# A hybrid attention and recurrence layer on one core: VectorE blocks kept in written order, and token projections that go one weight tile at a time

## The chip, the cores and the metric

The kernel runs on one core of a Trainium2 chip. The metric is the device time of one execution in microseconds (us); lower is better. Engines are named as in the profile: PE is TensorE's matmuls, PEld its weight loads, DVE is VectorE, ACT is ScalarE, POOL is GpSimd, SP is SyncE, which here issues nearly all DMAs.

## The reference, cut to what matters

One layer over 512 tokens of width 1024, in float32. The input is normalised and projected once; the columns of that projection feed two branches.

```python
xn = rmsnorm(h, norm_gain[i])
proj = xn @ w_in[i]
aq, ak, av, ag, bq, bf, bi, bg, gate_a, gate_b = jnp.split(proj, split_pts, axis=-1)
# attention: 8 heads of 64, QK norm, relative bias, causal within blocks
qa, ka = rmsnorm(heads(aq), q_norm_gain[i]), rmsnorm(heads(ak), k_norm_gain[i])
ya = moba_attention(qa, ka, va, rel_bias)...
ya = (ya * silu(ag)) @ w_up_a[i]
# recurrence: 4 heads, key and value width 128
log_f = log_sigmoid(fpre) + log1p(lb * exp(min(-fpre, 30)))
kb, qb, vb = (1 - lb) * sigmoid(-fpre), silu(bq), bi
#   cum = cumsum(log_f); scores[t, s] = sum_k q[t] k[s] exp(cum[t] - cum[s]); plus a carried state
yb = rmsnorm(hgrn2_chunkwise(qb, kb, vb, log_f), hgrn_out_gain[i])
yb = (yb * silu(bg)) @ w_up_b[i]
merged = sigmoid(gate_a) * ya + sigmoid(gate_b) * yb
h = h + merged @ w_out[i]
h = h + (p[i] @ w_ple[i]) * sigmoid(h @ w_ple_gate[i])
```

## The kernel before, in words

Every float32 operand of a large matmul is split into a high half (`wh`, `xh`, made by ACT, L184) and a low half (`wl`, `xl`, the DVE subtraction in L185), and a product is three matmuls: high by high, high by low, low by high. A weight tile is 128x1024 (512 KB): SP loads it into one of two buffers `wf`, and ACT and DVE write its halves into one of three buffers each (`wh`, `wl`). So the tile three further on may be written only when PE has read the last of this one. Weight tiles are numbered in the order of their use: 0 to 3 are `bi`, 4 to 7 `av`, 8 and 9 the first head's `bf` and `bq`, 10 to 13 `aq`, 14 to 17 `ak`, and so on.

A token projection (`proj_tok`: `bi`, `av`, `aq`, `ak`) has four PSUM banks, one for each 128 tokens (`t` from 0 to 3), and eight k slices of 128, two in each of four weight tiles. All projections take their banks in turn from one pool of four (`mm`). A bank's next user waits until the last reader of its old contents is done: `av` gets the banks of `bi`, which ACT evicts into `biv` (L397); `aq` gets two banks of `av` and then those of `bf` and `bq` of the first head. `bf` has its last reader in L422 of `hgrn_gates`. `bq` has its last reader in L431, the query gate `qm = sigmoid(bq) * bq` (tile `hq`).

For `bi`, the first projection, a function `between` feeds the tiles one by one. The other three take two tiles at a time: first all 24 matmuls of banks 0 and 1 on both tiles, then those of banks 2 and 3. One matmul of 128x512 is one row of the PE's order.

PE's order is the written one: a small clock in the program (`tick`, `cost`, `yield`) lets generators for the recurrence, the attention and the normalisation put their matmuls between those of the projections. On DVE, ACT, POOL and SP a list scheduler sets the order, by priority (`tc.high_priority(offset=AHEAD)` moves a block ahead) and by when it believes operands to be ready; inside `tc.manual_schedule(engines=...)` the program sets the order for the engines named.

The recurrence runs a head at a time: `hgrn_gates` (sigmoids, the scan `cum` in L428, the query gate), then `hgrn_intra`: first subtractions of `cum` (L447, L448, L460, L481, L484, L510), an `Exp` on ACT, a product on DVE, then small matmuls into two banks (`lpb`, `lpa`), from which DVE builds `s32` (L539 and seven predicated copies, L496) and ACT writes other parts of `sc`; four POOL copies (L556) bring `s32` into `sc`. Then `hgrn_out`: `hktp` (transposes), `hds` (the state), `hop` (the output, which reads `sc`), `hms` (its norm).

Of the kernel before, what the change touches and what calls it, by code (L numbers as in the profile page):

```python
# [14 lines left out]
AF = mybir.ActivationFunctionType  # L15
OP = mybir.AluOpType
# [5 lines left out]
NT = S // 128  # L22
# [18 lines left out]
LD = 2  # L41
# [9 lines left out]
AHEAD = 150  # L51
# [6 lines left out]
def hybrid_layer_kernel(  # L58
# [106 lines left out]
    eye = mkf[:, 0:32]  # L165
# [14 lines left out]
        A.activation(lb[:, 5], lb[:, 4], AF.Ln)  # L180


    def split(hi, lo, src):
        A.activation(hi, src, AF.Copy)  # L184
        V.tensor_tensor(lo, src, hi.bitcast(F32), op=OP.subtract)  # L185
# [36 lines left out]
    def w_split(upto):  # L222
        while len(wtile) <= min(upto, len(wseq) - 1):
            i = len(wtile)
            w_load(i)
            ap, kn, cols = wseq[i]
            hi = unit("wh", f"wh{i}", R, (128, kn, cols))
            lo = unit("wl", f"wl{i}", R, (128, kn, cols))
            with tc.high_priority(offset=AHEAD):
                split(hi, lo, wraw[i])  # L230
            wtile.append((hi, lo))

# [135 lines left out]
    def proj_tok(g, name, xh, xl, between=None):  # L368
        banks = [bank("mm", f"{name}{t}") for t in range(NT)]
        for kp in range(4):  # L370
            if between:
                between(kp)
                w2 = [weight(w_tok[g, kp], 0)]
                order = [(0, kk, t) for kk in range(2) for t in range(NT)]
                if kp == 3:
                    order = [(0, kk, t) for t in range(NT) for kk in range(2)]
            elif kp % 2 == 0:
                w2 = [weight(w_tok[g, kp]), weight(w_tok[g, kp + 1])]
                order = [(k2, kk, t) for t in (0, 1) for k2 in range(2) for kk in range(2)]
                order += [(k2, kk, t) for t in (2, 3) for k2 in range(2) for kk in range(2)]  # L380
            else:
                continue
            for k2, kk, t in order:
                wh, wl = w2[k2]
                k = 2 * (kp + k2) + kk
                s_ = slice(t * 128, t * 128 + 128)
                for i, (a, b) in enumerate(((xh[k], wh), (xl[k], wh), (xh[k], wl))):
                    PE.matmul(banks[t], a[:, s_], b[:, kk, :], start=(k == 0 and i == 0),  # L388
                              stop=(k == KD - 1 and i == 2))
                tick(0.681)  # L390
        return banks
# [19 lines left out]
    def hgrn_gates(h, F, Q):  # L411
        a = unit("H", f"ha{h}")
        A.activation(a, F, AF.Abs)
        A.activation(a, a, AF.Exp, scale=-1.0)
        A.activation(a, a, AF.Ln, bias=onec[:, 0:1])
        um = unit("H", f"hu{h}")
        V.tensor_scalar(um, F, -1.0, 30.0, op0=OP.mult, op1=OP.min)
        A.activation(um, um, AF.Exp)
        A.activation(um, um, AF.Ln, bias=onec[:, 0:1], scale=lbv[:, h:h + 1])
        V.scalar_tensor_tensor(a, F, 0.0, a, op0=OP.min, op1=OP.subtract)  # L420
        kb = unit("H", f"hk{h}")
        V.tensor_tensor(kb, a, F, op=OP.subtract)  # L422
        A.activation(kb, kb, AF.Exp, bias=ln1mlb[:, h:h + 1])
        V.tensor_tensor(a, a, um, op=OP.add)
        cum = um
        for c in range(NT):
            s_ = slice(c * 128, c * 128 + 128)
            V.tensor_tensor_scan(cum[:, s_], onec.to_broadcast([128, 128]), a[:, s_], 0.0, OP.mult, OP.add)  # L428
        sigmoid(a, Q)
        qm = unit("QM", f"hq{h}", shape=(128, 16, 48))  # L430
        V.tensor_tensor(qm[:, :, 0:32], a.rearrange("p (g t) -> p g t", t=32), Q.rearrange("p (g t) -> p g t", t=32),  # L431
                        op=OP.mult)
        hg[h] = (kb, qm, cum)

    def hgrn_intra(h):
# [3 lines left out]
        def halves(b):  # L439

            x = unit("Q", f"hx{h}_{b}")
            n = S // (2 * b)

            def v(t, half):
                return t.rearrange("p (n two b) -> p n two b", two=2, b=b)[:, :, half, :]
            ref = v(cum, 0)[:, :, b - 1:b].to_broadcast([128, n, b])
            V.tensor_tensor(v(x, 0), ref, v(cum, 0), op=OP.subtract)  # L447
            V.tensor_tensor(v(x, 1), v(cum, 1), ref, op=OP.subtract)  # L448
            A.activation(x, x, AF.Exp)
            V.tensor_tensor(v(x, 0), v(kb, 0), v(x, 0), op=OP.mult)  # L450
            xq = x.rearrange("p (n two g t) -> p n two g t", two=2, t=32, g=b // 32)[:, :, 1]
            qq = q.rearrange("p (n two g) t -> p n two g t", two=2, g=b // 32)[:, :, 1]
            V.tensor_tensor(xq, qq, xq, op=OP.mult)
            return x

        def near():

            c2 = cum.rearrange("p (g n two) -> p g n two", n=16, two=2)
            o = qm[:, :, 32:48]
            V.tensor_tensor(o, c2[:, :, :, 1], c2[:, :, :, 0], op=OP.subtract)  # L460
            A.activation(o, o, AF.Exp)
            V.tensor_tensor(o, q.rearrange("p g (n two) -> p g n two", two=2)[:, :, :, 1], o, op=OP.mult)

        def fours(b):


            kx = unit("Q", f"hkx{h}_{b}")
            qx = unit("QX", f"hqx{h}_{b}", shape=(128, 16, 48))
            n, m = S // (4 * b), 8 // b
            parts = [(d, 4 - d, e * b) for d, e in ((1, 0), (2, 3), (3, 5))]  # L470
            k4 = kx.rearrange("p (n f t) -> p n f t", f=4, t=b)
            c4 = cum.rearrange("p (n f t) -> p n f t", f=4, t=b)
            b4 = kb.rearrange("p (n f t) -> p n f t", f=4, t=b)
            q4 = q.rearrange("p g (m f t) -> p g m (f t)", m=m, f=4)
            x4 = qx.rearrange("p g (m e) -> p (g m) e", m=m)
            y4 = qx.rearrange("p g (m e) -> p g m e", m=m)
            G.memset(k4[:, :, 3, :], 0.0)

            def end(w):
                return c4[:, :, 0:w, b - 1:b].to_broadcast([128, n, w, b])  # L480
            V.tensor_tensor(k4[:, :, 0:3], end(3), c4[:, :, 0:3], op=OP.subtract)  # L481
            for d, w, e in parts:
                o = x4[:, :, e:e + w * b].rearrange("p n (f t) -> p n f t", t=b)
                V.tensor_tensor(o, c4[:, :, d:4], end(w), op=OP.subtract)  # L484
            A.activation(k4[:, :, 0:3], k4[:, :, 0:3], AF.Exp)
            A.activation(qx, qx, AF.Exp)
            V.tensor_tensor(k4[:, :, 0:3], b4[:, :, 0:3], k4[:, :, 0:3], op=OP.mult)
            for d, w, e in parts:
                o = y4[:, :, :, e:e + w * b]
                V.tensor_tensor(o, q4[:, :, :, d * b:4 * b], o, op=OP.mult)  # L490
            return kx, qx
# [15 lines left out]
        kd = unit("KT", f"hkd{h}", shape=(128, 3 * 128))  # L507
        cv = cum.rearrange("p (c t) -> p c t", c=NT)
        k3 = kd.rearrange("p (c t) -> p c t", c=3)
        V.tensor_tensor(k3, cv[:, 0:3, 127:128].to_broadcast([128, 3, 128]), cv[:, 0:3, :], op=OP.subtract)  # L510
        A.activation(kd, kd, AF.Exp)
        V.tensor_tensor(kd, kd, kb[:, :3 * 128], op=OP.mult)
        yield 2.5
# [22 lines left out]
            PE.matmul(lnr[p_, c, :], kb[:, o:o + 32], qm[:, 4 * c + g, :], start=True, stop=True)  # L536
        cost(1.5)
        A.activation(cum, cum, AF.Exp)
        V.tensor_tensor(s32, lnr[:, :, 0:32], eye[:, None, :].to_broadcast([128, NT, 32]), op=OP.mult)  # L539
        scv = sc.rearrange("p (i two) t -> p i two t", two=2)  # L540
        for par in range(2):
            i = 64 * par
            A.activation(scv[0:64, :, par, 64:128], big[i:i + 64, 0:2, :], AF.Copy)
            for half in range(2):
                j = 64 * half
                A.activation(scv[j:j + 32, :, par, j + 32:j + 64], big[i + 32 * half:i + 32 * half + 32, 2:4, 0:32], AF.Copy)
        for i, b in ((4, 8), (1, 2)):
            for d, e in ((1, 0), (2, 3), (3, 5)):
                pred(i + d - 1, lambda t: t.rearrange("p c (m e) -> p c m e", m=8 // b)[:, :, :, d * b:4 * b],
                     l4[b].rearrange("p c (m e) -> p c m e", m=8 // b)[:, :, :, e * b:(e + 4 - d) * b])  # L550
        pred(0, lambda t: t.rearrange("p c (n two) -> p c n two", two=2)[:, :, :, 1], lnr[:, :, 32:48])
        q12 = q[:, 4:16]
        V.tensor_tensor(q12, q12, cum[:, 128:].rearrange("p (g t) -> p g t", t=32), op=OP.mult)
        for g in range(4):
            s_ = slice(32 * g, 32 * g + 32)
            G.tensor_copy(sc[s_, :, s_], s32[s_])  # L556
        hg[h] += (kd,)

    def hgrn_out(h, vb):
        kb, qm, cum, kd = hg[h][:4]  # L560
        nk = 3 * 128
        yield 3.5
        kt = bank("g", f"hktp{h}")
        for c in range(3):
            PE.transpose(kt[:, c * 128:c * 128 + 128], kd[:, c * 128:c * 128 + 128], ident)
# [449 lines left out]
```

## Time and profile before

| | |
|---|---|
| device time, median of 3 runs | 473.75 us (473.31 to 473.81) |
| device time of the profiled execution | 474.0 us |
| its span, first to last instruction | 471.9 us |
| PE busy | 464.6 us (98%), 2776 records |
| DVE busy | 310.8 us (66%), 615 instructions |
| ACT busy | 273.9 us (58%), 479 instructions |
| POOL busy | 14.2 us (3%), 34 instructions |
| HBM read | 45.75 MB |

A matmul's end is modelled in the profile, and its rows overlap: a row of 0.39 us starts 0.227 us after the one before it. The distance between starts is what shows PE's rate. "Idle before" in brackets counts from the modelled end, so a wait is longer by some 0.16 us when it is measured from start to start. Times below are us from the start of the span.

### The profile page before, as it was taken

To read this page: it belongs to the slowest core of one execution; us is meant where nothing else is said; L and a number is where in the kernel's file an instruction comes from. 1 tells how busy PE (TensorE), PEld (TensorE's weight loads), DVE (VectorE), ACT (ScalarE), POOL (GpSimd) and SP (SyncE) were. 2 spreads that over 40 slices of the span, in tenths; PEclk is the share of its full clock that TensorE was granted. 3 is DMA by queue.
4 is the path that set the end of the run, shared out by engine and by line. 5 is a ranking of instruction groups with operands and counts; after the bars stand their busy time and mean duration, and the time that the engine had idled before them with its cause. 6 is when DMAs were issued, how large, how long until landed. Compare 5 with 4: busy or idle time off the path is not lost.

```text
span 471.9 us, 7256 instructions
## 1 busy us (share of the span) xinstructions
PE 464.6 (98%) x2776; PEld 384.8 (82%) x2776; DVE 310.8 (66%) x615; ACT 273.9 (58%) x479; POOL 14.2 (3%) x34
## 2 busy tenths in 40 slices
PE   9999999999999999999999999999999999999996
PEld 7888877888888778888788888888878888888886
DVE  4769696668989799849995466434459854543332
ACT  5857683478598789748885676554344522243201
POOL 0005000000000010000000100000000000000000
PEclk9999999999999999999999999999999999999999
DMA  7642222221541423231422233112534544322211
GB/s 228 218 145 90 90 89 90 89 90 50 172 145 59 141 85 90 90 111 47 131 91 92 90 101 102 47 62 53 188 95 138 193 145 147 109 93 95 91 44 46
DMA packets 19027, 50.42 MB, mean 107 GB/s; under 512 B 2352, under 2 KB 2992, under 8 KB 18992
## 3 DMA queue, kind: packets, MB, share of 16 engines
q1 hardware_dynamic: 18848, 49.95, 33.1%
q8 instruction: 22, 0.36, 0.3%
q14 instruction: 13, 0.11, 0.1%
q10 hardware_dynamic: 144, 0.01, 0.0%
HBM read 45.75 MB, written 2.10 MB: 101 GB/s over the span
## 4 chain that ended last, share of the span: by engine, by line
PE 87%; DVE 6%; ACT 5%; issue 1%; POOL 0%; DVEq 0%; POOLq 0%
PE ga L246 9%; PE g L246 9%; PE h L246 9%; PE gb L246 7%; PE bi L388 5%; PE ua L246 5%; PE ak L388 5%; PE ub L246 5%; PE av L388 5%; PE bg L246 5%; PE bf L246 4%; PE ag L246 3%; PE aq L388 3%; PE pe L246 2%; PE o L733 2%; PE s L700 2%
## 5 line engine op out<-in xcount | busy, mean ns | idle before, releaser
L184 ACT ACTIVATE wh<-wf 128x1024 fp32r<-128x1024 f32 (+1 forms) x81 | 77.5, 957 | 106.0 <-PE h L246 19.1
L185 DVE TENSOR_TENSOR wl<-wf,wh 128x1024 fp32r<-128x1024 f32 (+1 forms) x81 | 89.8, 1111 | 48.4 <-ACT wh L184 47.9
L707 DVE CUSTOM_DVE_ANT_0 p<-s,bias 128x128 f32<-128x128 f32 (+3 forms) x32 | 15.0, 486 | 21.8 <-PE s L700 21.7
L709 ACT ACTIVATE p<-p,ps 128x128 f32<-128x128 f32 (+3 forms) x32 | 17.7, 554 | 19.5 <-DVE ps L707 19.5
L246 PE MATMUL g<-hh,wh 128*128 128x512 f32 (+1 forms) x72 | 26.3, 365 | 0.0
L246 PE MATMUL g<-hl,wh 128*128 128x512 f32 (+1 forms) x72 | 26.3, 365 | 0.0
L246 PE MATMUL g<-hh,wl 128*128 128x512 f32 (+1 forms) x72 | 26.3, 365 | 0.0
L246 PE MATMUL gb<-xh,wh 128*128 128x512 f32 x64 | 26.3, 411 | 0.0
L246 PE MATMUL ga<-xh,wh 128*128 128x512 f32 x64 | 25.6, 400 | 0.0
L246 PE MATMUL gb<-xh,wl 128*128 128x512 f32 x64 | 25.1, 393 | 0.0
L246 PE MATMUL ga<-xh,wl 128*128 128x512 f32 x64 | 25.0, 391 | 0.0
L246 PE MATMUL gb<-xl,wh 128*128 128x512 f32 x64 | 25.0, 391 | 0.0
L246 PE MATMUL ga<-xl,wh 128*128 128x512 f32 x64 | 25.0, 390 | 0.0
L246 PE MATMUL h<-mh,wh 128*128 128x512 f32 x64 | 24.9, 390 | 0.0
L246 PE MATMUL h<-ml,wh 128*128 128x512 f32 x64 | 24.9, 389 | 0.0
L246 PE MATMUL h<-mh,wl 128*128 128x512 f32 x64 | 24.9, 389 | 0.0
L722 ACT ACTIVATE ptS<-pt 128x384 f32<-128x384 f32 (+1 forms) x24 | 12.5, 521 | 10.0 <-PE pt L718 9.8
L903 DVE TENSOR_TENSOR hf<-h,xres 128x512 f32<-128x512 f32 x8 | 5.5, 691 | 18.1 <-PE h L246 18.1
L246 PEld LDWEIGHTS g<-hh,wh 128*128 128x128 f32 x72 | 13.6, 189 | 2.2
L246 PEld LDWEIGHTS g<-hh,wl 128*128 128x128 f32 x72 | 13.6, 189 | 2.2
L246 PEld LDWEIGHTS g<-hl,wh 128*128 128x128 f32 x72 | 13.6, 189 | 2.1
L945 DVE TENSOR_TENSOR sg<-sg,pe 128x512 f32<-128x512 f32 (+1 forms) x9 | 5.6, 625 | 14.4 <-ACT sg L944 12.1
(319 smaller groups left out, 1265.2 us busy)
## 6 DMA issues: line engine op xcount, KB each, us to landing
wf<-in_w_tr_dram SPq DMA_DIRECT2D x32, 512.0 KB, 3.4
wf<-in_w_tok_dram SPq DMA_DIRECT2D x15, 512.0 KB, 3.3
wf<-in_w_up_dram SPq DMA_DIRECT2D x16, 256.0 KB, 2.7
wf<-in_w_o_dram SPq DMA_DIRECT2D x8, 512.0 KB, 3.3
wf<-in_w_g_dram SPq DMA_DIRECT2D x8, 512.0 KB, 3.3
bias<-in_brow_dram SPq DMA_DIRECT2D x8, 256.0 KB, 3.4
xres<-in_xT_dram SPq DMA_DIRECT2D x8, 256.0 KB, 2.8
xr<-in_xT_dram SPq DMA_DIRECT2D x7, 256.0 KB, 5.5
```

The source lines that it names most:

```text
L184: A.activation(hi, src, AF.Copy)
L185: V.tensor_tensor(lo, src, hi.bitcast(F32), op=OP.subtract)
L246: PE.matmul(ps, a[:, k, :], b[k], start=(n == 0), stop=(n == tot - 1))
L388: PE.matmul(banks[t], a[:, s_], b[:, kk, :], start=(k == 0 and i == 0), stop=(k == KD - 1 and i == 2))
L700: PE.matmul(sp[:, o:o + nk], qn[h][:, qs], k_[:, :nk], start=(i == 0), stop=(i == 1))
L707: V.tensor_tensor_reduce(p_, sp[:, o:o + nk], T[:, nk - 1::-1], -1.0, 3e38, OP.add, OP.min, st[:, 0:1])
L709: A.activation(p_, p_, AF.Exp, bias=st[:, 0:1], scale=-1.0, accum_out=st[:, 1:2])
L722: A.activation(pt, tp[:, :n * 128], AF.Copy)
L733: PE.matmul(o[64 * j:64 * j + 64, qs], va[kb][:, h0:h0 + 64], pts[2 * hp + j, i][:, o0 + kb * 128:o0 + kb * 128 + 128], start=(kb == 0), s ...
L903: V.tensor_tensor(t, ps, xres, op=OP.add)
L945: V.tensor_tensor(t[:, :w], t[:, :w], pe[:, s_], op=OP.mult)
```

## The change: three edits in the order of work

1. `proj_tok` takes one weight tile at a time also for `av`, `aq` and `ak`. The order inside a tile is k slice by k slice over all four banks; the last tile goes bank by bank.
2. A helper `in_order()` puts a few DVE instructions under `tc.manual_schedule`: the low halves of the weight tiles, the query gate, and the recurrence's first subtractions.
3. The end of `hgrn_intra` (from L539 to the POOL copies) gets high priority, with the product on `q12` (L553) moved behind the copies in the text; `hgrn_out` begins 5.0 us of the program's clock after it where it had 3.5.

```diff
+    def in_order():
+        return tc.manual_schedule(engines={mybir.EngineType.DVE})
...
-            with tc.high_priority(offset=AHEAD):
+            with tc.high_priority(offset=AHEAD), in_order():
                 split(hi, lo, wraw[i])
...
         for kp in range(4):
             if between:
                 between(kp)
-                w2 = [weight(w_tok[g, kp], 0)]
-                order = [(0, kk, t) for kk in range(2) for t in range(NT)]
-                if kp == 3:
-                    order = [(0, kk, t) for t in range(NT) for kk in range(2)]
-            elif kp % 2 == 0:
-                w2 = [weight(w_tok[g, kp]), weight(w_tok[g, kp + 1])]
-                order = [(k2, kk, t) for t in (0, 1) for k2 in range(2) for kk in range(2)]
-                order += [(k2, kk, t) for t in (2, 3) for k2 in range(2) for kk in range(2)]
-            else:
-                continue
-            for k2, kk, t in order:
-                wh, wl = w2[k2]
-                k = 2 * (kp + k2) + kk
+            wh, wl = weight(w_tok[g, kp], 0 if between else LD)
+            order = [(kk, t) for kk in range(2) for t in range(NT)]
+            if kp == 3:
+                order = [(kk, t) for t in range(NT) for kk in range(2)]
+            for kk, t in order:
+                k = 2 * kp + kk
...
-        V.tensor_tensor(qm[:, :, 0:32], a.rearrange("p (g t) -> p g t", t=32), Q.rearrange("p (g t) -> p g t", t=32),
-                        op=OP.mult)
+        with in_order():
+            V.tensor_tensor(qm[:, :, 0:32], a.rearrange("p (g t) -> p g t", t=32),
+                            Q.rearrange("p (g t) -> p g t", t=32), op=OP.mult)
...
-            V.tensor_tensor(v(x, 0), ref, v(cum, 0), op=OP.subtract)
-            V.tensor_tensor(v(x, 1), v(cum, 1), ref, op=OP.subtract)
+            with in_order():
+                V.tensor_tensor(v(x, 0), ref, v(cum, 0), op=OP.subtract)
+                V.tensor_tensor(v(x, 1), v(cum, 1), ref, op=OP.subtract)
...
         A.activation(cum, cum, AF.Exp)
-        V.tensor_tensor(s32, lnr[:, :, 0:32], eye[:, None, :].to_broadcast([128, NT, 32]), op=OP.mult)
+        with tc.high_priority(offset=AHEAD):
+            V.tensor_tensor(s32, lnr[:, :, 0:32], eye[:, None, :].to_broadcast([128, NT, 32]), op=OP.mult)
...
+            for g in range(4):
+                s_ = slice(32 * g, 32 * g + 32)
+                G.tensor_copy(sc[s_, :, s_], s32[s_])
         q12 = q[:, 4:16]
         V.tensor_tensor(q12, q12, cum[:, 128:].rearrange("p (g t) -> p g t", t=32), op=OP.mult)
-        for g in range(4):
-            s_ = slice(32 * g, 32 * g + 32)
-            G.tensor_copy(sc[s_, :, s_], s32[s_])
...
-        yield 3.5
+        yield 5.0
```

`near`, `fours` and the subtraction into `hkd` (L460, L481, L484, L510) get the same `in_order()` as the two lines shown.

Where the instructions stand. First PE, at the start of `aq` (banks `aq0` to `aq3`; `wh10` and `wh11` are the first two of its four weight tiles, `xh0` to `xh7` the k slices). Before:

```order
L388 MATMUL aq0_618<-wh10_536,xh0_390 128x512
...
L388 MATMUL aq0_618<-wh11_567,xh2_399 128x512
...
L388 MATMUL aq1_619<-wh10_536,xh0_390 128x512
...
L388 MATMUL aq2_620<-wh10_536,xh0_390 128x512
...
L388 MATMUL aq3_621<-wh10_536,xh0_390 128x512
```

Twelve rows lie from the first row of a bank to that of the next, so bank 3 is first written by the 37th matmul of `aq`. In the change (its lines stand three higher there):

```order
L385 MATMUL aq0_651<-wh10_560,xh0_399 128x512
L385 MATMUL aq0_651<-wh10_560,xl0_400 128x512
L385 MATMUL aq0_651<-wl10_561,xh0_399 128x512
L385 MATMUL aq1_652<-wh10_560,xh0_399 128x512
L385 MATMUL aq1_652<-wh10_560,xl0_400 128x512
L385 MATMUL aq1_652<-wl10_561,xh0_399 128x512
L385 MATMUL aq2_653<-wh10_560,xh0_399 128x512
L385 MATMUL aq2_653<-wh10_560,xl0_400 128x512
L385 MATMUL aq2_653<-wl10_561,xh0_399 128x512
L385 MATMUL aq3_654<-wh10_560,xh0_399 128x512
```

Bank 3 is now first written by the tenth matmul, bank 2 by the seventh. `av` and `ak` change in the same way.

Second DVE, in the first head, from the scan to the query gate. This is the change; the rows before read the same but for the line numbers (L510, L185, L484, L460, L512, L431):

```order
L425 SCALAR_TENSOR_TENSOR hu0_630<-onec_85,ha0_626 128x128 x4
L512 TENSOR_TENSOR hkd0_936<-hu0_630 128x384
L189 TENSOR_TENSOR wl12_658<-wf12_655,wh12_657 128x1024
L446 TENSOR_TENSOR hx0_64_713<-hu0_630 128x4x64
...
L485 TENSOR_TENSOR hqx0_8_820<-hu0_630 128x16x8
L460 TENSOR_TENSOR hq0_646<-hu0_630 128x16x16
L514 TENSOR_TENSOR hkd0_936<-hkd0_936,hk0_635 128x384
L429 TENSOR_TENSOR hq0_646<-ha0_626,bq0_601 128x16x32
```

The last row is the query gate, the last reader of `bq0`. It stands behind the same sixteen instructions as before: nothing moved here.

Third DVE, in the third head (`hq2`), where `s322` is that head's `s32` and `hqx3` and `hkd3` belong to the fourth. Before, from the fifth to the last of its seven predicated copies:

```order
L496 COPY_PREDICATED s322_1904<-mkf_69,lpa2_2185 128x16x4
...
L484 TENSOR_TENSOR hqx3_8_2612<-hu3_2336 128x16x8
L707 ISA p32_2301,ps32_2302<-s32_2298,bias3_1712 128x384
L460 TENSOR_TENSOR hq3_2352<-hu3_2336 128x16x16
L510 TENSOR_TENSOR hkd3_2705<-hu3_2336 128x384
L496 COPY_PREDICATED s322_1904<-mkf_69,lpa2_2185 128x16x2
L185 TENSOR_TENSOR wl36_2357<-wf36_2354,wh36_2356 128x1024
L577 COPY st2_2368<-hds2_2364 128x128
L496 COPY_PREDICATED s322_1904<-mkf_69,lpa2_2185 128x64
```

And in the change, from the fourth on:

```order
L497 COPY_PREDICATED s322_2056<-mkf_69,lpa2_2356 128x16x6
L460 TENSOR_TENSOR hq3_2494<-hu3_2478 128x16x16
L497 COPY_PREDICATED s322_2056<-mkf_69,lpa2_2356 128x16x4
L497 COPY_PREDICATED s322_2056<-mkf_69,lpa2_2356 128x16x2
L497 COPY_PREDICATED s322_2056<-mkf_69,lpa2_2356 128x64
L710 ISA p32_2466,ps32_2467<-s32_2463,bias3_1835 128x384
```

The predicated copies now stand nearly together, ahead of the attention's step and of the weight tile. On PE the matmuls `hktp`, `hds` and `hop` of a head stand some six to nine projection matmuls later against `lpb` than before.

More of the change, by code (lines that the diff above doesn't have):

```diff
@@ L459, in near @@
             o = qm[:, :, 32:48]
-            V.tensor_tensor(o, c2[:, :, :, 1], c2[:, :, :, 0], op=OP.subtract)
+            with in_order():
+                V.tensor_tensor(o, c2[:, :, :, 1], c2[:, :, :, 0], op=OP.subtract)
             A.activation(o, o, AF.Exp)
@@ L480, in end @@
                 return c4[:, :, 0:w, b - 1:b].to_broadcast([128, n, w, b])
[L481 to L484, printed above, removed]
+            with in_order():
+                V.tensor_tensor(k4[:, :, 0:3], end(3), c4[:, :, 0:3], op=OP.subtract)
+                for d, w, e in parts:
+                    o = x4[:, :, e:e + w * b].rearrange("p n (f t) -> p n f t", t=b)
+                    V.tensor_tensor(o, c4[:, :, d:4], end(w), op=OP.subtract)
             A.activation(k4[:, :, 0:3], k4[:, :, 0:3], AF.Exp)
@@ L509, in hgrn_intra @@
         k3 = kd.rearrange("p (c t) -> p c t", c=3)
-        V.tensor_tensor(k3, cv[:, 0:3, 127:128].to_broadcast([128, 3, 128]), cv[:, 0:3, :], op=OP.subtract)
+        with in_order():
+            V.tensor_tensor(k3, cv[:, 0:3, 127:128].to_broadcast([128, 3, 128]), cv[:, 0:3, :], op=OP.subtract)
         A.activation(kd, kd, AF.Exp)
@@ L538, in hgrn_intra @@
         A.activation(cum, cum, AF.Exp)
-        V.tensor_tensor(s32, lnr[:, :, 0:32], eye[:, None, :].to_broadcast([128, NT, 32]), op=OP.mult)
[L540 to L551, printed above, removed]
+        with tc.high_priority(offset=AHEAD):
+            V.tensor_tensor(s32, lnr[:, :, 0:32], eye[:, None, :].to_broadcast([128, NT, 32]), op=OP.mult)
+            scv = sc.rearrange("p (i two) t -> p i two t", two=2)
+            for par in range(2):
+                i = 64 * par
+                A.activation(scv[0:64, :, par, 64:128], big[i:i + 64, 0:2, :], AF.Copy)
+                for half in range(2):
+                    j = 64 * half
+                    A.activation(scv[j:j + 32, :, par, j + 32:j + 64], big[i + 32 * half:i + 32 * half + 32, 2:4, 0:32], AF.Copy)
+            for i, b in ((4, 8), (1, 2)):
+                for d, e in ((1, 0), (2, 3), (3, 5)):
+                    pred(i + d - 1, lambda t: t.rearrange("p c (m e) -> p c m e", m=8 // b)[:, :, :, d * b:4 * b],
+                         l4[b].rearrange("p c (m e) -> p c m e", m=8 // b)[:, :, :, e * b:(e + 4 - d) * b])
+            pred(0, lambda t: t.rearrange("p c (n two) -> p c n two", two=2)[:, :, :, 1], lnr[:, :, 32:48])
+            for g in range(4):
+                s_ = slice(32 * g, 32 * g + 32)
+                G.tensor_copy(sc[s_, :, s_], s32[s_])
         q12 = q[:, 4:16]
         V.tensor_tensor(q12, q12, cum[:, 128:].rearrange("p (g t) -> p g t", t=32), op=OP.mult)
-        for g in range(4):
-            s_ = slice(32 * g, 32 * g + 32)
-            G.tensor_copy(sc[s_, :, s_], s32[s_])
         hg[h] += (kd,)
```

## Prediction

> **What bounds the kernel now.** I read the page's busy shares first, then PE's own waits, then PE's rows in order of time around each wait, and last the DVE and ACT rows that end those waits.
>
> ```profile
> PE 464.6 (98%) x2776; PEld 384.8 (82%) x2776; DVE 310.8 (66%) x615; ACT 273.9 (58%) x479; POOL 14.2 (3%) x34
> PE aq L388 <- DVE wl L185: 0.9, 1, 0.9
> PE warm L147 <- PEq L1002: 0.8, 1, 0.8
> PE hop L586 <- POOL sc L556: 0.7, 1, 0.7
> PE hktp L565 <- DVE s L496: 0.5, 1, 0.5
> PE pt L718 <- DVE p L711: 0.4, 1, 0.4
> PE aq L388 <- DVE hq L431: 0.2, 1, 0.2
> 27.90:50.65 22.75, 22.75 (x103) 1.00 0.33 113
> 61.53:84.98 23.45, 22.36 (x97) 1.00 0.20 68
> 84.98:112.99 28.01, 28.01 (x265) 1.00 0.24 76
> ```
>
> PE is never without work for long: its waits sum to 3.5 us in six places. So a gain can hardly exceed 3 us, while a new wait of PE is paid in full, since no later slack takes it up. The three stretches are `av`, `aq` and `ak`. 96 matmuls at 0.227 us are 21.8 us; `av` holds two matmuls and four transposes besides, and has no wait; `aq` holds nothing else and loses 1.7 us; in `ak` the rest is recurrence and transposes.
>
> **The change, part one: four banks at once in `aq`.** Here are the first matmul of `aq`, the first of bank 3 (the 37th), and the place where the fourth weight tile is met:
>
> ```profile
> 61.53 0.39 PE L388 MATMUL aq<-wh,xh 128*128 128x512 f32 x1
> 61.76 0.39 PE L388 MATMUL aq<-wh,xl 128*128 128x512 f32 x1
> ...
> 69.47 0.39 PE L388 MATMUL aq<-wl,xh 128*128 128x512 f32 x1
> 70.01 0.50 PE L388 MATMUL aq<-wh,xh 128*128 128x512 f32 x1 [0.16 <-DVE hq L431]
> 70.35 0.39 PE L388 MATMUL aq<-wh,xl 128*128 128x512 f32 x1
> ...
> 74.46 0.39 PE L388 MATMUL aq<-wh,xl 128*128 128x512 f32 x1
> 75.78 0.50 PE L388 MATMUL aq<-wl,xh 128*128 128x512 f32 x1 [0.93 <-DVE wl L185]
> ```
>
> The wait at 70.01 shows who holds bank 3: it was the bank of `bq`, and the query gate L431 is its last reader. PE just about missed it, by 0.31 us (70.01 - 69.47 - 0.23). On DVE that gate ends late:
>
> ```profile
> 61.31 1.37 DVE L428 TENSOR_TENSOR_SCAN hu<-onec,ha 128x128 f32<-128x128 f32 x4
> ...
> 69.28 0.68 DVE L431 TENSOR_TENSOR hq<-ha,bq 128x512 f32<-128x512 f32 x1
> 64.43 0.63 ACT L253 ACTIVATE ha<-ha 128x512 f32<-128x512 f32 x1
> ```
>
> Its operand is ready at 65.06 (the ACT row), but it stands behind the scan and sixteen more instructions, which run without a gap, and ends at 69.96. By the order nothing of this moves. What moves is PE: bank 3 is met by the tenth matmul, at 61.53 + 9 x 0.227 = 63.57, and waits until 70.01: 6.44 us where it was 0.31. Bank 2 (the bank of `bf`) is met at 62.89; L422, its last reader, is before the scan and done. The 0.11 us by which the first matmul after a wait is longer (70.01 to 70.35) is paid once, where before it was paid twice. The other wait, 1.09 us at 74.46, goes: tile 10 is now let go after 24 matmuls instead of 48, and tile 13, the fourth, is first needed by the 73rd matmul, 63 behind the stall, 14.3 us. Its DVE half, for which PE waits until 75.78 here, does not move. Sum for `aq`: 6.44 + 0.11 against 0.31 + 0.11 + 1.09 + 0.11 (the 1.7 us above): **+4.9 us**.
>
> **`av`.** Its bank 3 is that of `bi`, and its reader is the ACT copy of L397:
>
> ```profile
> 27.90 0.39 PE L388 MATMUL av<-wh,gh 128*128 128x512 f32 x1
> 29.73 1.06 ACT L184 ACTIVATE wh<-wf 128x1024 fp32r<-128x1024 f32 x1 [1.25 <-DMA wf<-in_w_tok_dram]
> 30.70 0.58 ACT L397 ACTIVATE biv<-bi 128x512 f32<-128x512 f32 x1
> ```
>
> That copy is queued on ACT behind the high half of weight tile 6, which waits for its DMA, and ends at 31.28. The tenth matmul of `av` is due at 27.90 + 2.04 = 29.94. Before, bank 3 came with the 37th. The wait is 1.3 us, with the restart **+1.4 us**. Banks 1 and 2 are copied ahead of that tile and wait for nothing. The chain of the norm starts from `mp`, which stands behind 18 matmuls of `av` as before, so it moves with PE. In it `wl` of tile 7 now comes between L260 and L261, 1.2 us; I cost that at nothing, because its first user has room, 3.9 us here:
>
> ```profile
> 36.01 0.69 DVE L262 TENSOR_TENSOR rstd<-rstd,rtmp 128x512 f32<-128x512 f32 x1
> 40.65 0.60 PE L328 MATMUL mt<-ident,rstd 128*128 128x128 f32 x4
> 51.56 0.68 DVE L185 TENSOR_TENSOR xl<-xr,xh 128x512 fp32r<-128x512 f32 x1
> 55.64 0.39 PE L246 MATMUL bf<-xl,wh 128*128 128x512 f32 x1
> 85.92 0.58 ACT L636 ACTIVATE qr<-aq 128x512 f32<-128x512 f32 x1
> ```
>
> The last `xl` is done 3.4 us before `bf` meets it; were that cover gone, `bf` would wait for the excess alone.
>
> **`ak`.** The last row shows bank 3 of `aq` copied at 86.50, 1.5 us after `ak` begins (84.98); it is now needed after 2.0 us. It fits with half a microsecond to spare: **0**, at worst +0.5.
>
> **The recurrence's tail.** The wait of `hop` belongs to the third head:
>
> ```profile
> 225.41 0.49 PE L718 MATMUL pt<-ident,p 128*128 128x128 f32 x3
> 226.57 0.71 PE L586 MATMUL hop<-sc,biv 128*128 128x128 f32 x4 [0.67 <-POOL sc L556]
> 225.25 1.27 POOL L556 COPY sc<-s 32x128 f32<-32x128 f32 x4 [33.77 <-DVE s L496]
> ```
>
> Three transposes take about 0.3 us, so 0.8 us are lost there (1.16 - 0.33). The copies into `s32` now stand together and `hop` nine matmuls (2.0 us) later, so this goes: **-0.8 us**. The 0.5 us at `hktp` is mostly the modelled end and is left out. The wait of `pt` stays, since the second head's DVE rows do not change. The fourteen subtractions, the SP orders, where a weight load changes place with one neighbour, and the attention's steps, shifted by some 1.4 us against the weights, I cost at nothing: DVE is 66% busy and their users on PE come several microseconds later.
>
> **The clock after the long wait.** At both ends of the span PE shows what idleness does:
>
> ```profile
> 0.77 3.75 PE L147 MATMUL warm<-const-float32-1.0 128*128 128x128 f32 x16 [0.77 <-PEq L1002]
> 4.56 0.77 PE L388 MATMUL bi<-wh,gh 128*128 128x512 f32 x1
> 5.13 0.63 PE L388 MATMUL bi<-wh,gl 128*128 128x512 f32 x1
> 5.55 0.71 PE L388 MATMUL bi<-wl,gh 128*128 128x512 f32 x1
> 6.06 0.63 PE L388 MATMUL bi<-wh,gh 128*128 128x512 f32 x1
> 6.49 0.46 PE L388 MATMUL bi<-wh,gl 128*128 128x512 f32 x1
> 6.78 0.40 PE L388 MATMUL bi<-wl,gh 128*128 128x512 f32 x1
> 468.00:470.80 2.80, 0.07 (x1) 0.00 (x0) 0.84 (x2) 0.00 (x0) 0.00 (x0) 1.00 0.14 47
> 470.80:471.90 1.10, 0.00 (x0) 0.00 (x0) 0.00 (x0) 0.00 (x0) 0.00 (x0) 0.51 0.00 0
> ```
>
> PE's last matmul ends near 468.1, and from 470.8 the granted clock is about half: 2.7 us of idleness was enough. At the start matmuls come 0.42 to 0.57 us apart until 6.5, then 0.23 to 0.29: the full rate came 5.7 us after the first work. A wait of 6.4 us should therefore end at half rate. Its price lies between the 0.1 us after a wait of 0.9 us, and half of 5.7 us, 2.85. 6.4 us is nearer to the start, where PE had done nothing, so I take that, a little reduced, since two of the starts shown (0.57 and 0.51 apart, the others 0.42 and 0.43) held waits of their own: **+2.4 us**. The wait of 1.3 us in `av` is nearer to the 0.9 us one, and gets 0.1 (in the 1.4).
>
> The Trainium skill, TensorE: Matmul & The Clock Gate, Part 1 (The HAM clock gate) says that the array falls to half rate after one idle window of about 3.4 us and comes back after one busy window, and that the window runs freely. The trace agrees as far as it goes: half the clock at the end, and half the pace at the start. By the page's figures the half rate would last 3.4 to 6.8 us, which as an estimate is a loss of 1.7 to 3.4 us and keeps the sum.
>
> **Sum.** +4.9 + 1.4 - 0.8 + 2.4 = +7.9 us on a profiled execution of 474.0 us (span 471.9, 2.1 around it), so 481.9, span 479.8. The median lies 0.25 below that execution: **481.6 us**, 1.7% slower.
>
> **Rivals.** (A) The clock stays full, or nearly. For it: no row of this kernel shows the clock drop in the middle. Against it: the last two rows. It gives 479.2. (B) The other side: bank 3 of `aq` is free in time, because the gate comes earlier on the chip or PE waits for an earlier reader. Then `aq` has no wait at all, and the sum is 1.4 - 1.7 - 0.8 = -1.1: 472.7, faster. It decides from the point where the gate ends within 1.1 us of PE's arrival, at 64.7 of this trace's time. Against it: the gate's operand alone is ready only at 65.06, and the order leaves it behind sixteen instructions until 69.96. (C) The wait of 1.3 us in `av` already halves the clock: another 2.4, 484.0. For it: the start, where a PE that was busy most of the time from 0.77 on was not yet at full rate at 4.56. Against it: the wait of 1.09 us at 74.46 was followed by the full rate at once. (D) Small waits that I cost at nothing appear, `qr` in `ak`, `st` before `hop`, `hms`: up to 1.5 us, inside the range.
>
> **Chances.** My forecast with (D) 0.72, (A) 0.13, (C) 0.08, (B) and other ways to be no slower 0.07. The time is that of the first. The range takes in (A) and nearly (C): 479.0 to 483.8. The measurement of this kernel tells about 0.2% (0.9 us) from no change: slower by more than that 0.93, within it 0.03, faster 0.04.
>
> **What would show it.** In the changed profile: one row among PE's waits, `aq` for DVE `hq`, of some 6 us, at the tenth matmul of `aq` (near 71); a row of `av` for ACT `biv` of about 1.2; no `hop` for POOL and no `aq` for `wl`; PE's rows 0.43 us apart for some microseconds behind the long wait, and a granted clock below 1 in those slices. The first head's gate should start near 70.7. The prediction is wrong if the gate's wait is under 2 us, or if the stretch of `aq` stays near 23.5 us; its size is off if the half rate does not show.

## The result and the profile after

The changed kernel takes 480.13 us (median of 4 runs, 479.26 to 480.57) against 473.69 us before. That is 1.0134 times the time before (95% interval 1.0121 to 1.0146), or 6.4 us slower; 481.6 was forecast. The profiled execution took 480.57 us, with a span of 478.6.

The page's busy shares, and PE's own waits (us in total, times, longest us), of the changed kernel:

```profile
PE 466.1 (97%) x2776; PEld 386.5 (81%) x2776; DVE 311.9 (65%) x615; ACT 273.7 (57%) x479; POOL 15.2 (3%) x34
PE aq L385 <- DVE hq L429: 6.3, 1, 6.3
...
PE av L385 <- ACT biv L394: 0.4, 1, 0.4
PE hms L605 <- DVE htl L189: 0.2, 1, 0.2
```

The number of matmuls is the same. One long wait of 6.3 us is new, beside small ones of 0.4 us and less, and the waits of `aq` for `wl`, of `hop` for POOL and of `hktp` are gone. The stretches of `av`, `aq` and `ak` (length, PE busy, granted clock, DMA share, GB/s), which were 22.75, 23.45 and 28.01 us long:

```profile
27.78:51.16 23.38, 23.02 (x103) 1.00 0.33 108
62.05:92.97 30.92, 24.64 (x98) 0.89 0.20 68
92.97:120.94 27.97, 27.97 (x264) 1.00 0.24 76
```

`aq` alone is 7.5 us longer, and its mean clock is 0.89. Here are the ninth and tenth matmul of `aq`, the last slow ones, the first fast one, and the gate on DVE:

```profile
63.86 0.39 PE L385 MATMUL aq<-wl,xh 128*128 128x512 f32 x1
70.53 0.79 PE L385 MATMUL aq<-wh,xh 128*128 128x512 f32 x1 [6.28 <-DVE hq L429]
...
75.38 0.63 PE L385 MATMUL aq<-wl,xh 128*128 128x512 f32 x1
75.81 0.52 PE L385 MATMUL aq<-wh,xh 128*128 128x512 f32 x1
76.17 0.39 PE L385 MATMUL aq<-wh,xl 128*128 128x512 f32 x1
69.80 0.67 DVE L429 TENSOR_TENSOR hq<-ha,bq 128x512 f32<-128x512 f32 x1
```

The tenth matmul starts 6.67 us after the ninth, 6.44 more than the usual 0.227. The thirteen matmuls from 70.53 on take 5.64 us to the next start, 2.7 us more than at 0.227. Windows of 1 us show the granted clock (the number behind the bracket, 1.00 being full speed):

```profile
69.00:70.00 1.00, 0.00 (x0) 0.62 0.00 0
...
75.00:76.00 1.00, 1.00 (x4) 0.50 0.00 0
76.00:77.00 1.00, 1.00 (x6) 0.96 0.00 0
```

A mean of 0.62 says that 0.76 us of that microsecond were at half rate, so the clock fell at 69.24, with PE idle since 64.09. By the last row it rose at 76.08, 6.84 us later.

### The profile page after: what moved, and what is told of

Same layout as the page of the kernel before. It is cut to its first block, busy times and chain, and to the rows that moved or that the text cites. A ratio compares the mean times of both kernels' runs of the same rounds, so it can differ in the third digit from the quotient of the medians.

```text
span 478.6 us, 7248 instructions
## 1 busy us (share of the span) xinstructions
PE 466.1 (97%) x2776; PEld 386.5 (81%) x2776; DVE 311.9 (65%) x615; ACT 273.7 (57%) x479; POOL 15.2 (3%) x34
## 4 chain that ended last, share of the span: by engine, by line
PE 81%; ACT 7%; DVE 7%; DMA 3%; issue 1%; SPq 0%; DVEq 0%; ACTq 0%
PE ga L250 9%; PE g L250 9%; PE h L250 9%; PE gb L250 7%; PE aq L385 5%; PE ua L250 5%; PE ub L250 5%; PE av L385 4%; PE bf L250 4%; PE bg L250 4%; PE ag L250 3%; PE ak L385 3%; DMA wf<-in_w_tok_dram 3%; PE bq L250 2%; PE pe L250 2%; ACT wh L188 2%
## 5 line engine op out<-in xcount | busy, mean ns | idle before, releaser
L250 PE MATMUL g<-hh,wh 128*128 128x512 f32 (+1 forms) x72 | 26.3, 365 | 0.0
L250 PE MATMUL g<-hl,wh 128*128 128x512 f32 (+1 forms) x72 | 26.3, 365 | 0.0
L250 PE MATMUL g<-hh,wl 128*128 128x512 f32 (+1 forms) x72 | 26.3, 365 | 0.0
L385 PE MATMUL aq<-wh,xh 128*128 128x512 f32 x32 | 13.7, 428 | 6.3 <-DVE hq L429 6.3
```

The lines of the kernel that those rows point to most:

```text
L250: PE.matmul(ps, a[:, k, :], b[k], start=(n == 0), stop=(n == tot - 1))
```

## The experiments

**1. The tiles alone.** The kernel before, with the new `proj_tok` loop and nothing else of the change.

> The kernel before, with the tile-by-tile token projections alone; DVE in-order blocks and the recurrence's end as before. Theory (the whole loss comes from this part: 0.6 us in av, 6.4 us of waiting for the query gate and 2.7 us of half rate in aq, less the 1.6 us that aq waited before; the rest of the change gives 1.5 us back): aq lasts about 30.9 us, the one long wait is 6.3 us at its tenth matmul, and the time is 480.13 + 1.5 = 481.6 us, 481.0 to 482.2. Rival (the DVE in-order blocks hold the gate back, and the tiles alone are cheap): no wait over 3 us in aq, and a time under 477.

Measured: 481.33 us, ratio 1.0156 (1.0142 to 1.0170). PE's waits:

```profile
PE aq L381 <- DVE hq L424: 6.3, 1, 6.3
PE av L381 <- ACT biv L390: 1.4, 1, 1.4
...
PE hop L579 <- POOL sc L549: 0.7, 1, 0.7
PE hktp L558 <- DVE s L489: 0.5, 1, 0.5
```

The whole loss is in this loop; the in-order blocks do not hold the gate back. The waits of `hop` and `hktp` stay, since the end of the recurrence is the old one here.

**2. Everything but the tiles.** The changed kernel with the old loop over pairs.

> The changed kernel, with the token projections in pairs of tiles as before; in-order blocks and the new end of the recurrence stay. Theory: the two waits of aq are back (0.3 and 1.1 us between starts), none for the gate of over 1 us, no half rate; the third head's wait for POOL stays away; 473.69 - 1.5 = 472.2 us, 471.7 to 472.8. Rival (in-order blocks cost time by themselves): slower than 473.7 us.

Measured: 471.87 us, 0.9963 (0.9951 to 0.9976), 1.85 us faster than before; `aq` is 23.45 us long again. So the change consists of a loss of 8.3 us (480.13 - 471.87) and a gain of 1.85. Taken the other way, by experiment 1, the rest of the change is worth 1.2 us (481.33 - 480.13); the difference is within the spread of those runs.

**3. The query gate first.** In the changed kernel, for the first head, the subtractions are issued behind the query gate on DVE:

```diff
-        V.tensor_tensor(qm[:, :, 0:32], ...)
+        gate[h] = V.tensor_tensor(qm[:, :, 0:32], ...)
...
+    def behind(h):
+        return tc.issue_after(gate[h].ins) if h == 0 else in_order()
...
-            with in_order():        # the four places in hgrn_intra
+            with behind(h):
```

> The changed kernel, with the first head's subtractions issued behind its query gate on DVE, so that the gate stands right behind the scan and one weight half; PE's order is the same. Theory: the gate starts when its operand from ACT is ready (65.06 us before, here some 65.6), ends near 66.3, and PE waits 2.2 us at the tenth matmul instead of 6.4. Whether 2.2 us of idleness also lower the clock is open: the half rate at the end of the span came after 2.7 us. If it does not: 4.2 + 2.7 less, 473.2 us; if it does: 475.9. Rival (the wait at the tenth matmul is not for the gate but for something that ends with it, such as the weight half or a semaphore of the scan): wait of over 5 us as before, 479 to 480.5.

Measured: 474.41 us, 1.0023 (1.0013 to 1.0033). The gate on DVE, and the ninth to eleventh matmul of `aq`:

```profile
66.14 0.69 DVE L433 TENSOR_TENSOR hq<-ha,bq 128x512 f32<-128x512 f32 x1 [0.99 <-ACT ha L257]
64.67 0.39 PE L385 MATMUL aq<-wl,xh 128*128 128x512 f32 x1
66.89 0.50 PE L385 MATMUL aq<-wh,xh 128*128 128x512 f32 x1 [1.83 <-DVE hq L433]
67.22 0.39 PE L385 MATMUL aq<-wh,xl 128*128 128x512 f32 x1
```

The gate now waits for ACT and not in DVE's queue, and the wait between starts is 2.0 us. PE's order is the same, so what held bank 3 is the gate's place on DVE. In this execution there is no half rate behind 2.0 us (the next starts are 0.33 and 0.23 us apart). The time is 1.2 above the 473.2 forecast; `av` is 24.41 us long here, 1.0 more than in the traced execution of the change (experiment 9 shows why it varies). Of ten runs six lie at 473.9 to 474.4, with a mean granted clock of 0.999 to 1.0, and four at 475.4 to 476.0, with 0.996. The traced execution of experiment 5, with one stretch of 3.42 us at half rate, also has 0.996. So the four most likely had such a stretch as well. None of them was traced. It more likely stood behind the 2.0 us of `aq` than behind the wait in `av`: in experiments 4 and 9, which take `av` tile by tile too and have no wait over 1.1 us in `aq`, all 17 runs have 0.998 or more.

**4. No idleness in the stall.** Ahead of the tenth matmul, in the changed kernel:

```diff
             for kk, t in order:
+                if g == 0 and (kp, kk, t) == (0, 0, 3):
+                    fill = bank("g", "fill")
+                    for _ in range(28):
+                        PE.matmul(fill, xh[0][:, 0:128], wh[:, 0, :], start=True, stop=True)
```

> The changed kernel, with 28 more matmuls of 128x512 (6.35 us at 0.227 us) ahead of the tenth matmul of aq, into a spare bank that nobody reads: the stall is as long, but PE is not idle in it. Theory (the half rate comes from the idleness): matmuls behind the wait come 0.227 us apart at once, granted clock 1 there, the wait shrinks to 0.1 to 0.3 us, and the time is 2.6 us less, 477.5 us. Rival (the slow dozen of matmuls comes from something else, such as the weight tiles or bank contention with DVE): the matmuls behind stay 0.43 us apart and the time stays at 480.1.

Measured: 479.16 us (477.55 to 480.04), 1.0111 (1.0093 to 1.0128). The profiled execution (480.04):

```profile
64.69 6.51 PE L385 MATMUL fill<-wh,xh 128*128 128x512 f32 x28
71.13 0.50 PE L389 MATMUL aq<-wh,xh 128*128 128x512 f32 x1
71.47 0.39 PE L389 MATMUL aq<-wh,xl 128*128 128x512 f32 x1
PE s L707 <- DMA kl<-kl: 0.4, 1, 0.4
PE s L707 <- DMA kh<-kh: 0.4, 1, 0.4
kh<-kh SPq DMA_DIRECT2D x2, 128.0 KB, 7.1
```

The mechanism is as forecast: full pace behind the stall, a mean clock of 1.0, and `aq` (with the fillers) 28.35 us instead of 30.92, 2.6 less. In all five runs the mean granted clock is 0.999 or 1.0, where the changed kernel has 0.992 or 0.993. The median time fell by only 1.0, a miss. In the profiled execution `av` was 24.26 us, 0.9 longer, and the attention's `s` lost 1.2 us from start to start to the transfers of `kh` and `kl`, which makes up the difference there; the other four were not traced. The last row is the DMA issues of 125 to 146 us, us to landing: 7.1, where the changed kernel has this in the same window:

```profile
kh<-kh SPq DMA_DIRECT2D x2, 128.0 KB, 5.6
```

The fastest run, 477.55, is where the forecast of 477.5 lies.

**5. Bank 3 last.** In the first tile of `aq` bank 3 comes after the other three (changed kernel):

```diff
+            if g == 0 and kp == 0:
+                order = [(kk, t) for kk in range(2) for t in range(3)] + [(0, 3), (1, 3)]
```

> The changed kernel, where the first weight tile of aq takes bank 3 after the other three, so that bank 3 is met by the 19th matmul instead of the tenth. Theory: the gate ends where it did, so nine matmuls (2.04 us) move from behind the wait to ahead of it, and the wait between starts is 4.4 us instead of 6.44; 4.4 us are more than the 2.7 us of the end of the span, so the half rate still follows: 480.1 - 2.0 = 478.1 us. Rival (the half rate needs a longer idleness than 4.4 us): matmuls 0.227 us apart behind the wait, 475.5 us.

Measured: 477.31 us, 1.0081 (1.0066 to 1.0097).

```profile
66.72 0.39 PE L387 MATMUL aq<-wl,xh 128*128 128x512 f32 x1
71.35 0.61 PE L387 MATMUL aq<-wh,xh 128*128 128x512 f32 x1 [4.25 <-DVE hq L431]
71.00:72.00 1.00, 0.65 (x2) 0.80 0.00 0
75.00:76.00 1.00, 1.00 (x5) 0.99 0.00 0
```

The wait is 4.40 us, as expected, and the half rate follows, but for half as long: from 71.60 to 75.02, 3.42 us, where the changed kernel had 6.84. It costs 1.7 us instead of 2.7; the time is 0.8 below the forecast, which had put it at 2.7. The profiled execution took 478.88 us and is the slowest of the six; `av` took 24.10 us in it, and `s` lost 0.5 to the transfer of `kl`. Five of the six have a mean granted clock of 0.996. The sixth (478.72 us) has 0.991, the mean of experiment 6's trace, where the half rate lasts twice as long.

**6. Half of the stall filled.** As experiment 4, with 14 matmuls instead of 28.

> The changed kernel with 14 matmuls (3.17 us) into a spare bank ahead of the tenth matmul of aq: PE works for half of the stall and is idle for the other half, 3.27 us. The wait between starts is 3.27 us and aq is of the same length but for the clock. Theory (idleness of 2.7 us or more is followed by the half rate): 13 matmuls slowed, 480.1 us and aq 30.9 us. Rival (the idleness has to fill a window of about 3.4 us, as the grid of the clock records, 3.41 us, suggests): full rate behind it, aq 28.3 us, 477.5 us.

Measured: 482.02 us, 1.0151 (1.0121 to 1.0181); three runs of 481.9 to 482.4 and one of 478.30.

```profile
63.48 3.33 PE L385 MATMUL fill<-wh,xh 128*128 128x512 f32 x14
69.92 0.80 PE L389 MATMUL aq<-wh,xh 128*128 128x512 f32 x1 [3.11 <-DVE hq L433]
70.51 0.63 PE L389 MATMUL aq<-wh,xl 128*128 128x512 f32 x1
69.00:70.00 1.00, 0.08 (x1) 0.54 0.00 0
75.00:76.00 1.00, 1.00 (x4) 0.55 0.00 0
PE s L707 <- DMA kh<-kh: 1.2, 1, 1.2
```

Here 3.26 us of idleness, from 66.66 on, were enough. The clock fell at 69.08, 2.4 us after the last filler, and rose at 75.90, 6.82 us later; `aq` took 31.1 us. So the rival falls, by which PE has to be idle for a full window of 3.4 us. But such a wait does not always do it: the run of 478.30 has a mean granted clock of 1.0, so it kept full rate, and the other three have 0.991 to 0.995. In the profiled execution (482.15) `s` also lost 1.9 us from start to start, 1.3 to the transfer of `kh` and 0.6 to that of `kl`.

**7 and 8. The two halves of the gain.** First the new end of `hgrn_intra` with `yield 5.0` alone, in the kernel before.

> The kernel before, with the new end of the recurrence alone (priority, product moved, 5.0 instead of 3.5 us of the program's clock); no in-order blocks, old token projections. The old tiles with the rest of the change took 471.87 us. Theory (the new end takes the waits of hop for POOL, 0.9 us, and of hktp for DVE, 0.7 us, away): 471.9 us, 471.5 to 472.4, neither wait in the profile. Rival (the in-order blocks do it): 473.7 us and both waits still there.

Measured: 474.21 us, 1.0012 (1.0004 to 1.0021): no gain, rather 0.5 us lost. The waits of `hop` for POOL and of `hktp` went, as expected, and others came:

```profile
PE hop L589 <- DVE st L581: 1.3, 1, 1.3
...
PE hds L574 <- ACT p L710: 0.6, 1, 0.6
...
228.96 2.10 DVE L490 TENSOR_TENSOR hqx<-hq,hqx 128x384 f32<-128x384 f32 x6
230.98 0.42 DVE L462 TENSOR_TENSOR hq<-hq 128x256 f32<-128x256 f32 x1
231.43 0.35 DVE L581 SCALAR_TENSOR_TENSOR st<-st,hu,hds 128x128 f32<-128x128 f32 x1
```

In the third head the last update of the state `st` stands behind seven products of the fourth head on DVE, and the last matmuls of `hop` wait for it. In experiment 2 both updates stand together:

```profile
227.55 0.73 DVE L590 SCALAR_TENSOR_TENSOR st<-st,hu,hds 128x128 f32<-128x128 f32 x2
```

Then the in-order blocks alone, with the old end and the old tiles:

> The kernel before, with the in-order blocks alone; the recurrence's end and the token projections as before, so PE's order is the same. The new end alone gave nothing (474.21 us): hop waited for DVE st there. Theory (neither part gains alone: the blocks move the third head's subtractions behind its predicated copies on DVE, but hop still stands early on PE and POOL's copies still come after the product on q12): the waits of hktp or hop get shorter but do not go, 473.0 us, 472.4 to 473.7. Rival (the blocks alone carry the gain): 471.9 us, no wait of hop for POOL.

Measured: 472.69 us, 0.9981 (0.9972 to 0.9989), 0.95 us faster. Here `hop` no longer waits for POOL, a wait that the theory had left in place in part; `hktp` still waits. Its wait, and the last predicated copy of the third head, here and then in the kernel before:

```profile
PE hktp L574 <- DVE s L504: 0.5, 1, 0.5
221.75 0.29 DVE L504 COPY_PREDICATED s<-mkf,lpa 128x64 f32<-128x64 int32 x1
...
224.83 0.29 DVE L496 COPY_PREDICATED s<-mkf,lpa 128x64 f32<-128x64 int32 x1
```

With the fourth head's subtractions kept back, the copies end 3.1 us earlier, and POOL begins 3.1 us earlier (222.18 instead of 225.25).

So the blocks bring half of the 1.85 us. The new end brings the other half, and only together with them.

**9. The price of `av` and `ak`.** The changed kernel with `aq` alone in pairs.

> The changed kernel with aq alone in pairs of tiles; av and ak stay tile by tile. Against the kernel with all three in pairs (471.87 us) this is the price of av and ak. Theory: av waits for the ACT copy of bank 3, 0 to 1.6 us as the DMA of weight tile 6 lands early or late (the traces so far show starts 0.5, 1.2, 1.4 and 1.6 us late, and one in time), ak costs nothing: 472.9 us, 472.3 to 473.6, with a wider spread of the runs. Rival (tile by tile also slows ak or the stretches behind): 474 or more.

Measured: 473.00 us (472.55 to 474.49), 0.9992 (0.9983 to 1.0000); 1.1 us above experiment 2; its runs spread over 1.9 us, those of experiment 2 over 0.7. In its profiled execution `av` does not wait at all. Here is the ACT copy of bank 3 first in this kernel, then in experiment 1, with the ninth to eleventh matmul of `av` there:

```profile
28.94 0.58 ACT L405 ACTIVATE biv<-bi 128x512 f32<-128x512 f32 x1
...
30.71 0.58 ACT L390 ACTIVATE biv<-bi 128x512 f32<-128x512 f32 x1
29.52 0.39 PE L381 MATMUL av<-wl,gh 128*128 128x512 f32 x1
31.34 0.50 PE L381 MATMUL av<-wh,gh 128*128 128x512 f32 x1 [1.44 <-ACT biv L390]
31.68 0.39 PE L381 MATMUL av<-wh,gl 128*128 128x512 f32 x1
```

The copy ends between 29.5 and 31.3, by the weight tile ahead of it, and PE is due at about 29.8: `av` loses 0 to 1.6 us from run to run. Behind these 1.6 us the clock holds (the next starts are 0.34 and 0.23 us apart). What moves is the point at which SP issues that tile's transfer: 24.6 us in this kernel's trace, 25.4 in that of the change, 26.3 in experiment 1.

**10. A version that beats both.** The gate of experiment 3, the order of experiment 5, `av` in pairs as before, `ak` tile by tile.

> A version meant to beat both: the changed kernel with av in pairs of tiles as before, aq tile by tile with bank 3 last in its first tile, and the first head's query gate ahead of its subtractions. Theory: the gate ends near 66, bank 3 is met at 61.7 + 4.1 = 65.8, so aq waits 0.3 us at most and lasts 21.8 to 22.2 us where the old tiles took 23.45; against 471.87 us that is 1.3 to 1.6 less: 470.4 us. Rival (the weight half of the fourth tile is late all the same, since its cause is DVE and not the hold on the first tile): a wait of some 1 us for wl is back in aq, and the time is 471.5 us.

Measured: 470.74 us, 0.9943 (0.9931 to 0.9954). The stretch of `aq`, the gate, and the 19th matmul of `aq`, which is the first on bank 3:

```profile
61.79:83.64 21.85, 21.85 (x97) 1.00 0.30 97
65.08 0.69 DVE L446 TENSOR_TENSOR hq<-ha,bq 128x512 f32<-128x512 f32 x1 [1.00 <-ACT ha L257]
65.87 0.46 PE L398 MATMUL aq<-wh,xh 128*128 128x512 f32 x1
```

`aq` takes 21.85 us, which is the time of its 96 matmuls: the tile-by-tile order does save the 1.6 us that `aq` lost before, if bank 3 is free when PE comes. No `wl` is late.

## Why the prediction was right

- **`aq`, the wait (+4.9): right.** The wait is 6.44 us from start to start at the tenth matmul, the figure forecast, since both ends of it moved together by 0.5. The `wl` wait went. Experiment 3 shows by DVE's order alone that it is the gate's place there. Rival (B), bank 3 free in time, is what experiment 10 makes true, and it decides as forecast: then `aq` has no wait.
- **`aq`, the clock (+2.4): right, and a little small.** It is 2.7 us with the restart, and experiment 4 takes it away by keeping PE busy. Rival (A), a full clock, is out. That the size was near is in part luck: the prediction took the 5.7 us of half rate at the start of the span for the length, and PE worked at half rate for 5.55 us here (70.53 to 76.08), but only for 3.42 in experiment 5 (71.60 to 75.02), behind a wait that was shorter by 2.0. The prediction had nothing that tells the two lengths apart. The Trainium skill, TensorE: Matmul & The Clock Gate, Part 1 (The HAM clock gate), has a free-running window of about 3.4 us, from which the prediction had estimated a loss of 1.7 to 3.4 us; the half rate of 3.42, 6.82 and 6.84 us agrees with such a grid. By that page the clock falls after an idle window of about 3.4 us; here the measurement differs, for in experiment 6 it fell 2.4 us after the last matmul.
- **`av` (+1.4): right place, size not fixed.** The loss is 0.6 us in the profiled execution, 0 to 1.6 in the others, and 1.1 by the medians of experiments 9 and 2 (with `ak` and small waits). The working took the ACT row of one trace for a constant, but that row hangs on a transfer that SP issues at different times. So the first head's gate started at 69.80, not near 70.7. Rival (C), a half clock behind `av`, did not come: experiment 1 has full pace behind 1.6 us, and the changed kernel shows one half-rate stretch, in `aq`.
- **The recurrence's end (-0.8): mis-sized, and its causes mixed up.** Measured: -1.85. The wait of `hktp`, left out as mostly the modelled end, is in the second head of the kernel before:

```profile
167.86 0.34 PE L700 MATMUL s<-kl,qs 128*128 128x384 f32 x1
168.71 0.52 PE L565 MATMUL hktp<-ident,hkd 128*128 128x128 f32 x3 [0.51 <-DVE s L496]
```

  That is 0.85 us between starts, where the next matmul otherwise starts 0.17 us after this row (142.05 to 142.22 in the same trace), so 0.7 us were lost; the new end takes them away (experiment 7) and the blocks do not. For `hop` the prediction named two things, the copies into `s32` together and `hop` nine matmuls later. The first is enough, and the in-order blocks alone bring it about (second part of experiments 7 and 8). Their subtractions the prediction had costed at nothing; yet without them the later `hop` only changes its wait for POOL into one for `st`.
- **`ak` (0): right**, 27.97 us against 28.01. Of the small waits of (D) one came, `hms` for `htl`, 0.25 us more than before.

With the sizes found the sum is 7.5 + 1.1 - 1.85 = 6.75 us against 6.4 measured. The forecast of 7.9 was 1.5 too high, 1.0 of it from the end of the recurrence.

## What to carry to other kernels

Taking tiles one by one over all accumulators makes each accumulator due early: list for each bank its last reader, when that ends, and which matmul first writes it, before and after. By the mean clocks, an idle stretch of TensorE cost more than its length here in every run with 4.4 or 6.4 us, in three of four with 3.3, and probably in four of ten with 2.0. So a long wait is worth shortening even where it can't be removed. An edit of the order on one engine may be worth something only together with one on another; try each alone, and both.

## What was not expected of the hardware

- In the traces the granted clock fell 2.4 to 5.2 us after PE's last matmul (experiment 6, the changed kernel), in experiment 5 even 0.25 us after PE had begun again, and did not fall behind 2.0 us (experiment 3). The half rate then lasted 3.42 or about 6.83 us, and a longer wait did not make it longer: 3.26 us of idleness cost 2.9 us beside its length, 6.44 cost 2.7, and 4.40 only 1.7. Two runs of one kernel can differ in it: in experiment 6 one of four kept full rate.
- The transfers of `kh` and `kl` within SBUF landed in 5.6 us in the changed kernel and in 7.1 in experiment 4, almost the same program, and PE lost 1.2 us by it, with no change near them. In the kernel before they took 2.7 us. Why they vary is not shown.
